# Keys and values as seven half-size products from the fourth attention unit on, the input sums two at a time in the first two units, and lambda folded into the scaling of the second softmax map

## The chip, the cores and the metric

The kernel runs on one core of one Trainium2 chip. The metric is the device time of one execution in microseconds. The kernel before takes 712.08 us, the median of 3 runs (711.63 to 712.46).

## The reference, cut to what matters

The block has 528 positions (16 meta tokens and 512 of the sequence), a width of 1024 and float32 data. A layer norm gives `h`; one projection `w_in` gives queries, keys, values and gates of two attention branches:

```python
proj = jnp.einsum('bld,dn->bln', h, w_in[i])
q_d, k_d, v_d, g_d, q_s, k_s, v_s, g_s, m_d, m_s = jnp.split(proj, IN_OFFSETS, axis=-1)
# differential attention: 8 heads, two softmax maps each
p = jax.nn.softmax(s, axis=-1)
a = p[:, :, 0] - lam * p[:, :, 1]
y_d = jnp.einsum('bhqk,bhkd->bhqd', a, v)
# stick-breaking attention: 16 heads, products of (1 - sigmoid) from the right
```

The two branches are normed, gated, projected, merged by sigmoid gates, projected once more and normed with the residual. Only the keys and values of the two branches and the line `a = ...` are touched here.

## The kernel before

**Numbers as pairs.** Each float32 operand of a large product is split into a high part, rounded to the matmul's format, and a low part, the rest. ScalarE (ACT) writes the high part of a weight tile (`wh`, L183), VectorE (DVE) the low part (`wl`, L188), and TensorE (PE) adds three products: high by high, high by low, low by high. A weight item is a tile of 128 x 4 x 128 and costs one ACT and one DVE instruction on 512 columns. `prep` does that for the item that is four ahead of the one that TensorE is to use.

**Units.** Attention goes through 16 units, u = 0 to 15: the 8 differential heads, then 8 pairs of stick-breaking heads. While the attention of unit u runs, TensorE also projects the keys and values of unit u+1 and the queries of unit u+2, so that small attention products and long projections lie between each other. A query (or gate) projection is 24 matmuls on 512 columns (L494 to L496).

**Two ways to the keys and values.** Up to the unit `SEVEN - 1` the keys (`stage_k`) and the values (`stage_v`) of a unit are two plain projections: 2 halves of the positions x 8 slices x 3 products each, 96 matmuls on 264 columns in all (L510). From unit `SEVEN` on `stage_kv` computes both together: the 2 x 2 blocks of (keys, values) by (first, second half of the positions) come from seven half-size products in place of eight, as in Strassen's scheme in Winograd's form: 7 x 4 x 3 = 84 matmuls on 264 columns (L690), with some sums before and behind them. Its weight sums are made by DMAs of GpSimd (POOL) that add into the tiles `rawk` (L146) and by one DVE addition (L169); it prepares seven weight items in place of four.

**Input sums.** The seven products also need four sums of the blocks of `h`. `input_sums(k)`, k = 0 to 3, makes a quarter of them: one small POOL copy (L660), four DVE operations on 264 columns (L662 to L665, in the tiles `hF`), one ACT cast into `tS` (L667) and one DVE subtraction on 1056 columns into `tl` (L668). The second of the seven products reads all four quarters of `tS` and `tl`. Before, with `SEVEN = 5`, the quarters are made one in each of the units u = 0 to 3, and the first seven products run in u = 4.

**Scores of a differential head.** For each of the 4 query blocks, last block first, and each of the two maps, TensorE fills a score bank `sc` (L754; there are two such banks), DVE adds the bias, takes the minimum and moves the scores to the map's tile `e` (L834), and ACT takes the exponential and its row sum `zs` (L838). Then DVE takes the reciprocals `rz` (L842), multiplies that of the second map by `nlam`, which is -lambda (L843, one column), scales the first map (L844) and adds the scaled second map to it (L845), which gives `apad`. TensorE transposes `apad` (L766, into `t`), ACT and DVE split the transposes (`ah`, `al`), and TensorE multiplies by the values (`av`).

**What sets the order.** Inside a unit `run(proj, steps)` walks through the projections and calls each step when the walk has come to the step's time (a number such as 8.0 on a scale of some 15 a unit). From u = 0 up to the end of the attention that is the order in which instructions are written, not the order in which they are issued: a scheduler places them afterwards, engine by engine, by its own estimate of when each is ready, and each engine then works through its list in that order. `placed` ties a few of them to the instructions written just before.

Of the kernel before, what the change touches and what calls it, by code (L numbers as in the profile page):

```python
# [35 lines left out]

ORDERED = [mybir.EngineType.PE, mybir.EngineType.DVE, mybir.EngineType.Activation, mybir.EngineType.Pool]
WARM = 14
SEVEN = 5
TD = [(0.85, 11.0, 14.5), (0.95, 13.0, 16.5)]  # L40
GATE_AT = {4: 0, 5: 1, 6: 2, 7: 3, 8: 4, 11: 5, 14: 6}
LO, HI = slice(0, 64), slice(64, 128)
# [3 lines left out]
def hybrid_block_kernel(ctx: ExitStack, tc: tile.TileContext, x, meta, emb_g, emb_b, w_in, b_gate,  # L46
# [175 lines left out]
    def placed(work, engines=ORDERED):  # L222

        ins = nc.cur_bb.bb.instructions
        n = len(ins)
        work()
        for e in engines:
            new = next((i for i in ins[n:] if i.engine == e), None)
            old = next((ins[m] for m in range(n - 1, max(n - 400, 0), -1) if ins[m].engine == e), None)
            if new is not None and old is not None:  # L230
                follow(new, old)
# [349 lines left out]
    with tc.tile_pool(name="att", bufs=1) as ap:  # L581
# [75 lines left out]
        def input_sums(k):  # L657


            g.tensor_copy(hP[k][:, :, :M], hM[:, k:k + 5:4])  # L660
            b11, b12, b21, b22 = [hP[k][:, m, ts(n, H2)] for m in range(2) for n in range(2)]
            v.tensor_tensor(b22, b12, b22, op=ALU.subtract)  # L662
            v.tensor_tensor(b12, b11, b12, op=ALU.subtract)
            v.tensor_tensor(b11, b22, b11, op=ALU.subtract)
            v.tensor_tensor(b21, b11, b21, op=ALU.add)  # L665
            h, l = tS[0][:, k:k + 5:4], pair_of("tl", F32R)
            s.copy(h, hP[k])  # L667
            v.tensor_tensor(l, hP[k], h.bitcast(F32), op=ALU.subtract)  # L668
            tL.append(l)
# [139 lines left out]
        def d_scores(unit, h):  # L809

            A = unit["A"]


            bias = ap.tile([P, L], F32, tag="bias", name="bias", bufs=2)
            if h == 0:
                g.iota(bias, pattern=[[-1, L]], base=400, channel_multiplier=1, allow_small_or_imprecise_dtypes=True)
                g.affine_select(bias, bias, pattern=[[-1, L]], compare_op=ALU.is_ge, fill=1e30, base=400,
                                channel_multiplier=1)
            g.tensor_scalar(bias, biases[-1] if h else bias, 0.5 if h else -0.5, None, op0=ALU.mult)
            biases.append(bias)  # L820
            a = apads[h % 2]
            mn = ap.tile([P, NB, 2, 2], F32, tag="mn", name="mn", bufs=2)
            zs = ap.tile([P, NB, 2], F32, tag="zs", name="zs", bufs=2)
            rz = ap.tile([P, NB, 2], F32, tag="rz", name="rz", bufs=2)
            for i in reversed(range(NB)):
                nk = NKEY[i]
                e = [E[c][:, ZOFF[i]:ZOFF[i] + nk] for c in range(2)]
                for c in range(2):
                    m = mn[:, i, c, :]
                    for n, (ps, k0, use) in enumerate(logits(A[c], K[c], i)):  # L830
                        if n == 1:
                            yield
                        b0 = 384 - P * i + k0
                        v.tensor_tensor_reduce(e[c][:, k0:k0 + use], ps[:, :use], bias[:, b0:b0 + use], -1.0, 3e38,  # L834
                                               ALU.add, ALU.min, m[:, n:n + 1])
                    if nk > 512:
                        v.tensor_tensor(m[:, 0:1], m[:, 0:1], m[:, 1:2], op=ALU.min)
                    s.activation(e[c], e[c], AF.Exp, scale=-1.0, bias=m[:, 0:1], accum_out=zs[:, i, c:c + 1])  # L838
                    if c == 0:
                        yield  # L840
                r = rz[:, i, :]
                v.reciprocal(r, zs[:, i, :])  # L842
                v.tensor_scalar(r[:, 1:2], r[:, 1:2], nlam, None, op0=ALU.mult)  # L843
                v.tensor_scalar(e[0], e[0], r[:, 0:1], None, op0=ALU.mult)  # L844
                v.scalar_tensor_tensor(a[:, AOFF[i]:AOFF[i] + nk], e[1], r[:, 1:2], e[0], op0=ALU.mult, op1=ALU.add)  # L845
                yield

        def d_values(unit, ta):
# [105 lines left out]
        for u, (kind, n) in enumerate(UNITS):  # L954
            unit = units[u]
            if u + 3 == SEVEN:
                pools["rawk"] = ap
            last = u + 1 == len(UNITS)
            proj = [] if last else keys_values(units[u + 1], *UNITS[u + 1])
            if u + 2 < len(UNITS):  # L960
                proj.append(stage_q(units[u + 2], *UNITS[u + 2]))
            steps = pending + [(0.6, lambda unit=unit: values(unit, kind))]
            pending = []
            if u + 1 < SEVEN:
                steps.append((9.2, store_k))
            if u in range(SEVEN - 5, SEVEN - 1):
                if not tS:
                    tS.append(ypool.tile([P, KT, L], F32R, tag="ys", name="tS"))
                steps.append((8.0, lambda k=u + 5 - SEVEN: placed(lambda: input_sums(k))))
            if u in GATE_AT and u < 14:  # L970
                proj.append(raw_gate(GATE_AT[u], kept["r"][GATE_AT[u]]))
            if kind == "d":
                ta = {}
                dt, t0, t1 = TD[u in GATE_AT]
                steps += spread(d_scores(unit, n), 0.0, dt, 10)
                parts = transposed(ta, apads[n % 2])
                steps += [(t0 + 0.7 * m, f) for m, f in enumerate(parts)]
                steps.append((t1, lambda: d_values(unit, ta)))
                pending = [(3.0 if n < 7 else 5.8, lambda unit=unit, n=n: d_norm(unit, n))]
            else:  # L980
                if n == 0:
                    diag.append(ap.tile([P, L], F32, tag="bias", name="diag", bufs=2))
                    g.memset(diag[0], 0.0)
                    g.tensor_copy(diag[0][:, L - P:], ident)
                    g.memset(v3[:, 1], 0.0)
                    for a in apads:
                        for i in range(NB):
                            g.memset(a[:, ds(AOFF[i] + NKEY[i] - 1, 1)], 0.0)
                if last:
                    ydT = [pair_of("ydT", n=S) for k in range(4)]  # L990
                    ydT = [ydT[k % 4][:, k // 4, :] for k in range(8)]
                    ysT = ypool.tile([P, 8, S], F32, tag="ys", name="ysT")
                    ysT = [ysT[:, k, :] for k in range(8)]
                    unit["y"] = ysT[7]

                    def fill_in(y, of):
                        placed(lambda: nc.sync.dma_start(y, of), [mybir.EngineType.SP])

                    fill_in(ydT[7], kept["d"][7])
                    for m, (y, of) in enumerate(((ydT, "gd"), (ysT, "gs"))):  # L1000
                        for j in range(7):
                            steps.append((1.3 + 1.5 * (7 * m + j), lambda o=y[j], x=kept[of][j]: fill_in(o, x)))
                    proj += [gate("d", n, lambda: ydT[7]), merge_gate(0, 0), merge_gate(0, 1), merge_gate(0, 2),
                             gate("s", n, lambda: ysT[7])]
                else:
                    if GATE_AT.get(u) == n:
                        yd = gpool.tile([P, S], F32, tag="sg", name="yd")
                        nc.sync.dma_start(yd, kept["d"][n])
                        proj.append(gate("d", n, lambda yd=yd: yd, kept["gd"][n]))
                    else:  # L1010
                        steps += zip((12.0, 24.0), late_gate(ap, *(kept[x][n] for x in ("d", "r", "gd"))))
                    proj.append(gate("s", n, lambda unit=unit: unit["y"], kept["gs"][n]))
                for c in range(2):
                    ta = {}
                    steps += spread(s_scores(unit, c, n == 0), (2.0 + 4.3 * c) if n == 0 else 4.4 * c, 0.85, 5)
                    parts = transposed(ta, apads[c])
                    times = LAST[c] if last else [7.0 + 6.5 * c + 0.7 * m for m in range(3)] + [10.5 + 6.5 * c]
                    steps += zip(times, parts)
                    steps.append((times[3], lambda c=c, ta=ta: s_values(unit, c, n, ta)))
                if last:  # L1020
                    steps.append((LAST[0][0] - 0.1, lambda: state.update(ends=len(nc.cur_bb.bb.instructions))))
            run(proj, steps)
# [236 lines left out]
```

## Time and profile before

| | before |
|---|---|
| median of 3 runs | 712.08 us |
| the profiled execution: its own time | 712.22 us |
| the profiled execution: span from first to last instruction | 710.4 us |
| granted TensorE clock, mean | 0.995 |
| busy in the span: PE, DVE, ACT, POOL | 697.5, 571.8, 439.2, 125.6 us |
| start of the units u = 1, 2, 3, 4, 5 on TensorE (first matmul of the next unit's keys) | 59.49, 83.54, 107.59, 131.66, 159.79 us |

A row of instruction groups gives line, engine, operation, output and inputs, shape, count, then busy time, the mean duration of one in ns, and the idle time of the engine just before. A row of stretches gives for each engine the busy time and the count, then the granted clock, the share of the DMA engines' time and GB/s. A row of the timeline gives start, duration, engine, line, operation, names, shape and count. A duration reaches from an instruction's start to its end; on TensorE and VectorE the next one starts before that end, so what an instruction costs in a dense stretch is the step from start to start.

### The profile page before, as it was taken

To read this page: it belongs to the slowest core of one execution; us is meant where nothing else is said; L and a number is where in the kernel's file an instruction comes from. 1 tells how busy PE (TensorE), PEld (TensorE's weight loads), DVE (VectorE), ACT (ScalarE), POOL (GpSimd) and SP (SyncE) were. 2 spreads that over 40 slices of the span, in tenths; PEclk is the share of its full clock that TensorE was granted. 3 is DMA by queue.
4 is the path that set the end of the run, shared out by engine and by line. 5 is a ranking of instruction groups with operands and counts; after the bars stand their busy time and mean duration, and the time that the engine had idled before them with its cause. 6 is when DMAs were issued, how large, how long until landed. Compare 5 with 4: busy or idle time off the path is not lost.

```text
span 710.4 us, 13389 instructions
## 1 busy us (share of the span) xinstructions
PE 697.5 (98%) x4494; PEld 636.9 (90%) x4494; DVE 571.8 (80%) x1265; ACT 439.2 (62%) x1065; POOL 125.6 (18%) x143
## 2 busy tenths in 40 slices
PE   9999999999999999999999999999999999999994
PEld 8999999989999898988989998988889998999884
DVE  6888897878787777988878889976666788788897
ACT  5766676757667587776857777666455546455300
POOL 3214210212222111212123120000012102220002
PEclk9999999999999999999999999999999999999997
DMA  9368754879888876899897976646576748795902
GB/s 293 93 169 164 167 133 125 184 181 183 198 200 184 201 177 164 186 215 214 200 217 174 206 171 175 166 133 197 178 174 112 164 123 182 133 198 170 322 15 104
DMA packets 182182, 123.36 MB, mean 174 GB/s; under 512 B 9009, under 2 KB 165074, under 8 KB 182114
## 3 DMA queue, kind: packets, MB, share of 16 engines
q1 hardware_dynamic: 148130, 102.32, 50.1%
q0 software_dynamic: 33664, 19.14, 21.6%
q10 hardware_dynamic: 320, 1.06, 0.4%
q8 instruction: 35, 0.57, 0.3%
q14 instruction: 33, 0.27, 0.1%
HBM read 91.96 MB, written 9.44 MB: 143 GB/s over the span
## 4 chain that ended last, share of the span: by engine, by line
PE 86%; DVE 6%; DMA 3%; ACT 2%; issue 1%; POOL 1%; SPq 0%; ACTq 0%; DVEq 0%; POOLq 0%
PE q L690 16%; PE ps L496 12%; PE ps L494 12%; PE ps L495 12%; PE q L1065 10%; PE ps L510 7%; PE sc L754 6%; PE t L766 4%; DMA lgb<-in_ln_b_dram 1%; PE bank L385 1%; PE tv L723 1%; DVE hr L1215 1%; DMA xt<-in_x_dram 1%; PE av L922 1%; DMA raw<-in_w_out_dram 1%
## 5 line engine op out<-in xcount | busy, mean ns | idle before, releaser
L188 DVE TENSOR_TENSOR wl<-raw,wh 128x512 fp32r<-128x512 f32 x169 | 115.7, 691 | 43.7 <-ACT wh L183 42.2
L494 PE MATMUL ps<-hTh,wh 128*128 128x512 f32 x368 | 145.0, 394 | 0.0
L495 PE MATMUL ps<-hTl,wh 128*128 128x512 f32 x368 | 144.5, 393 | 0.0
L496 PE MATMUL ps<-hTh,wl 128*128 128x512 f32 x368 | 144.4, 392 | 0.0
L183 ACT CAST wh<-raw 128x512 fp32r<-128x512 f32 x169 | 104.4, 625 | 28.0 <-PE ps L495 15.3
L496 PEld LDWEIGHTS ps<-hTh,wl 128*128 128x128 f32 x368 | 69.2, 188 | 13.9
L495 PEld LDWEIGHTS ps<-hTl,wh 128*128 128x128 f32 x368 | 69.2, 188 | 13.1
L494 PEld LDWEIGHTS ps<-hTh,wh 128*128 128x128 f32 x368 | 69.2, 188 | 12.9
L146 POOL DMA_DIRECT2D rawk<-in_w_in_dram x44 | 60.8, 1642 | 96.9 <-DMA rawk<-in_w_in_dram 58.4
L754 PE MATMUL sc<-k,A 128*128 128x264 f32 (+3 forms) x320 | 65.9, 299 | 0.1
L1065 PE MATMUL q<-gh,wh 128*128 128x256 f32 x224 | 63.5, 283 | 0.2 <-ACT t L1074 0.2
L1065 PE MATMUL q<-gl,wh 128*128 128x256 f32 x224 | 63.4, 283 | 0.0
L1065 PE MATMUL q<-gh,wl 128*128 128x256 f32 x224 | 63.4, 283 | 0.0
L907 DVE TENSOR_TENSOR_SCAN e<-e,diag 128x528 f32<-128x528 f32 (+1 forms) x64 | 53.4, 848 | 7.5 <-ACT e L901 7.3
L754 PEld LDWEIGHTS sc<-k,A 128*128 128x128 f32 x320 | 50.3, 189 | 3.3 <-ACT e L901 0.3
L690 PE MATMUL q<-tS,wh 128*128 128x264 f32 x176 | 50.9, 290 | 0.9 <-DVE low L612 0.9
L690 PE MATMUL q<-tl,wh 128*128 128x264 f32 x176 | 50.2, 286 | 0.0
L690 PE MATMUL q<-tS,wl 128*128 128x264 f32 x176 | 50.2, 286 | 0.0
L510 PE MATMUL ps<-hTh,wh 128*128 128x264 f32 x160 | 46.4, 290 | 0.2 <-ACT k L632 0.2
L933 POOL DMA_DIRECT2D ys<-half x14 | 11.8, 840 | 195.9 <-ACT ys L932 119.2
L510 PE MATMUL ps<-hTh,wl 128*128 128x264 f32 x160 | 45.6, 286 | 0.0
L510 PE MATMUL ps<-hTl,wh 128*128 128x264 f32 x160 | 45.5, 285 | 0.0
(291 smaller groups left out, 1851.4 us busy)
## 6 DMA issues: line engine op xcount, KB each, us to landing
raw<-in_w_in_dram SPq DMA_DIRECT2D x141, 256.0 KB, 3.3
rawk<-in_w_in_dram POOLq DMA_DIRECT2D x44, 256.0 KB, 6.0
rawk<-in_w_in_dram SPq DMA_DIRECT2D x33, 256.0 KB, 3.9
k<-ks SPq DMA_DIRECT2D x60, 132.0 KB, 3.1
raw<-in_w_out_dram SPq DMA_DIRECT2D x16, 256.0 KB, 3.9
k<-ks SPq DMA_DIRECT2D x60, 66.0 KB, 2.8
A<-low SPq DMA_DIRECT2D x28, 128.0 KB, 2.8
raw<-in_w_br_diff_dram SPq DMA_DIRECT2D x12, 256.0 KB, 4.7
```

The lines of the kernel that those rows point to most:

```text
L146: second[l] = [lambda raw=raw, x=x: g.dma_start(raw, x, accum_op=ALU.add) for x in more]
L183: s.copy(wh, raw)
L188: eng.tensor_tensor(wl, raw, wh.bitcast(F32), op=ALU.subtract)
L494: pe.matmul(ps, wh[:, k % 4, :], hTh[:, k, M:], start=(k == 0), stop=False)
L495: pe.matmul(ps, wh[:, k % 4, :], hTl[:, k, M:], start=False, stop=False)
L496: pe.matmul(ps, wl[:, k % 4, :], hTh[:, k, M:], start=False, stop=(k == KT - 1))
L510: pe.matmul(ps[:, :H2], a[:, k % 4, :], b[:, k, ts(c, H2)], start=(k == 0 and m == 0), stop=(k == KT - 1 and m == 2))
L690: pe.matmul(bank, a[:, k, :], b, start=start and k == 0 and j == 0, stop=k == 3 and j == 2, skip_group_check=not start)
L754: pe.matmul(ps[:, :n], q, K[:, m, k0:k0 + n], start=(m == 0), stop=(m == 1))
L766: pe.transpose(t[:, o:o + P], a[:, AOFF[i] + j * P:AOFF[i] + (j + 1) * P], ident)
L907: v.tensor_tensor_scan(rev, rev, diag[0][:, L - nk:][:, ::-1], 0.0, ALU.mult, ALU.max)
L1065: pe.matmul(bank, a[:, k, :], b[:, n, k, :], start=start and k == 0 and m == 0, stop=k == 3 and m == 2, skip_group_check=not start)
```

## The change

`SEVEN` goes from 5 to 3: the keys and values of units 3 and 4 come from seven products too, so that the first seven products run in u = 2. The input sums are made two in u = 0 and two in u = 1, at 8.0 and 12.5 on the scale of the unit. In the scores, the second map is scaled by one operation with two factors (its reciprocal and `nlam`), and the first map is scaled in the addition; the one-column multiplication is gone.

```diff
-SEVEN = 5
+SEVEN = 3
...
                 v.reciprocal(r, zs[:, i, :])
-                v.tensor_scalar(r[:, 1:2], r[:, 1:2], nlam, None, op0=ALU.mult)
-                v.tensor_scalar(e[0], e[0], r[:, 0:1], None, op0=ALU.mult)
-                v.scalar_tensor_tensor(a[:, AOFF[i]:AOFF[i] + nk], e[1], r[:, 1:2], e[0], op0=ALU.mult, op1=ALU.add)
+                v.tensor_scalar(e[1], e[1], r[:, 1:2], nlam, op0=ALU.mult, op1=ALU.mult)
+                v.scalar_tensor_tensor(a[:, AOFF[i]:AOFF[i] + nk], e[0], r[:, 0:1], e[1], op0=ALU.mult, op1=ALU.add)
                 yield
...
             if u + 1 < SEVEN:
                 steps.append((9.2, store_k))
-            if u in range(SEVEN - 5, SEVEN - 1):
+            if u + 1 < SEVEN:
                 if not tS:
                     tS.append(ypool.tile([P, KT, L], F32R, tag="ys", name="tS"))
-                steps.append((8.0, lambda k=u + 5 - SEVEN: placed(lambda: input_sums(k))))
+                steps += [(8.0 + 4.5 * k, lambda k=2 * u + k: placed(lambda: input_sums(k))) for k in range(2)]
```

The scheduler makes new lists of all engines from this. First TensorE in u = 2. Before, the head of that unit's list reads (`ps` is the bank of the keys' plain projection, `sc` a score bank of unit 2, `t0` and `t1` transposes of unit 1; tiles carry their numbers):

```order
L510 MATMUL ps_1313<-hTh_149,wh_1112 128x264
L754 MATMUL sc_1330<-k0_448,A0_962 128x264 x2
L754 MATMUL sc_1334<-k0_448,A0_962 128x264 x2
L510 MATMUL ps_1313<-hTl_150,wh_1112 128x264
L510 MATMUL ps_1313<-hTh_149,wl_1113 128x264
L510 MATMUL ps_1313<-hTh_149,wh_1112 128x264
L510 MATMUL ps_1313<-hTl_150,wh_1112 128x264
L510 MATMUL ps_1313<-hTh_149,wl_1113 128x264
L766 MATMUL t0_1226<-ident_129,apad1_434 128x128 x4
L784 MATMUL t1_1238<-ident_129,sx_1224 128x128
L766 MATMUL t1_1238<-ident_129,apad1_434 128x128 x3
L510 MATMUL ps_1313<-hTh_149,wh_1112 128x264
```

Two score banks, and then projection matmuls again; the other scores of the unit follow one or two at a time up to its end. Now, a little behind the same place (the first of these rows comes after three quarters of the second of the seven products):

```order
L852 MATMUL av_1304<-ah0_1246,V_1018 128x512
L754 MATMUL sc_1444<-k0_448,A0_979 128x400 x2
L766 MATMUL t2_1270<-ident_129,apad1_434 128x128 x3
L754 MATMUL sc_1455<-k1_449,A1_980 128x400 x2
L754 MATMUL sc_1479<-k0_448,A0_979 128x272 x2
L723 MATMUL tv_1361<-ident_129,vT_1128 128x128 x4
L754 MATMUL sc_1501<-k1_449,A1_980 128x272 x2
L754 MATMUL sc_1515<-k0_448,A0_979 128x144 x2
L853 MATMUL av_1304<-af3_1278,v3_436 128x128
```

No projection matmul lies between these. The piece goes on with the other products by the values, and ends so (`q_1335` and `q_1336` are banks of the seven products, `ms` the norm of unit 1, `tl_1288` the last quarter of the input sums):

```order
L727 MATMUL t4_1367<-ident_129,sx_1368 128x128
L754 MATMUL sc_1537<-k1_449,A1_980 128x144 x2
L690 MATMUL q_1335<-tS_631,wh_1183 128x264
L875 MATMUL ms_1432<-sqh_1319,onesm_142 128x512
L876 MATMUL ms_1432<-sql_1320,onesm_142 128x512
...
L690 MATMUL q_1336<-hTh_149,wl_1292 128x264
L690 MATMUL q_1335<-tl_1288,wh_1183 128x264
```

From the first score bank of unit 2 (`sc_1351`) to the matmul that reads `tl_1288` stand all the 10 score banks, transposes and products of one unit's attention, but only 20 matmuls of the seven products: 7 behind `sc_1351`, one ahead of the norm, and 12 behind it.

On VectorE the last quarter of the input sums stood before in u = 3, a unit ahead of the first seven products (`hF_178` are its blocks, `tl_1883` its result, `sc_1829` to `sc_1858` scores of unit 3):

```order
L665 TENSOR_TENSOR hF_178<-hF_178 128x264
L834 ISA e1_447,mn_1682<-sc_1829,bias_1680 128x272
L834 ISA mn_1682 128x1
L732 TENSOR_TENSOR V_1700<-tv_1695,V_1700 128x384
L736 TENSOR_TENSOR v4_435<-t4_1701,v4_435 128x128
L870 TENSOR_TENSOR sql_1655<-sq_1652,sqh_1654 128x512
L612 SCALAR_TENSOR_TENSOR low_1663<-ps_1566,A0_1661 128x512
L668 TENSOR_TENSOR tl_1883<-hF_178,tS_631 128x1056
```

Now it stands in u = 2, behind all the scores of that unit (`sc_1537` is the tenth of its ten score banks):

```order
L665 TENSOR_TENSOR hF_178<-hF_178 128x264
L844 SCALAR_TENSOR_TENSOR apad0_433<-e0_446,rz_1350,e1_447 128x400
L843 TENSOR_SCALAR e1_447<-e1_447,rz_1350,nlam_146 128x272
L834 ISA e1_447,mn_1348<-sc_1537,bias_1346 128x144
L834 ISA mn_1348 128x1
L732 TENSOR_TENSOR V_1366<-tv_1361,V_1366 128x384
L736 TENSOR_TENSOR v4_435<-t4_1367,v4_435 128x128
L869 TENSOR_TENSOR sql_1320<-sq_1317,sqh_1319 128x512
L612 SCALAR_TENSOR_TENSOR low_1328<-ps_1230,A0_1326 128x512
L844 SCALAR_TENSOR_TENSOR apad0_433<-e0_446,rz_1350,e1_447 128x272
L668 TENSOR_TENSOR tl_1288<-hF_178,tS_631 128x1056
```

The steps of u = 1 at 8.0 and 12.5 thus lie a unit apart on VectorE: those of the third quarter in u = 1, together with those of the second, which were written in u = 0, and those of the fourth in u = 2.

## The prediction

> **What bounds the kernel now.** I read the page first: the span, the engines' shares, and the chain of work that ended last.
>
> ```profile
> span 710.4 us, 13389 instructions
> PE 697.5 (98%) x4494; PEld 636.9 (90%) x4494; DVE 571.8 (80%) x1265; ACT 439.2 (62%) x1065; POOL 125.6 (18%) x143
> PE 86%; DVE 6%; DMA 3%; ACT 2%; issue 1%; POOL 1%; SPq 0%; ACTq 0%; DVEq 0%; POOLq 0%
> ```
>
> TensorE is busy for 98% of the span and holds 86% of the chain. A busy TensorE can still hide waits, so I looked at stretches next, one for each of the units u = 1, 2, 3 (stretch, length, then busy time and count of PE, PEld, DVE, ACT, POOL, then clock, DMA share, GB/s).
>
> ```profile
> 59.49:83.54 24.05, 24.05 (x172) 22.82 (x171) 19.97 (x61) 16.00 (x43) 7.47 (x7) 1.00 0.83 159
> 83.54:107.59 24.05, 24.05 (x172) 22.83 (x171) 20.31 (x61) 16.36 (x43) 3.11 (x2) 1.00 0.76 167
> 107.59:131.66 24.07, 24.07 (x172) 22.83 (x171) 20.73 (x62) 16.38 (x43) 3.13 (x2) 1.00 0.56 141
> ```
>
> Three units with the same matmuls take the same 24.05 us to 0.02, without an idle moment of TensorE, while the other engines' load differs. So TensorE's own list is the bound in these units, VectorE has about 4 us of 24 to spare, and ScalarE 8. Last, the timeline, for what one matmul costs in a dense stretch: the first and the last row of 25 projection matmuls on 264 columns in a row, and of 11 on 512 columns.
>
> ```profile
> 121.41 0.28 PE L510 MATMUL ps<-hTl,wh 128*128 128x264 f32 x1
> ...
> 124.31 0.28 PE L510 MATMUL ps<-hTl,wh 128*128 128x264 f32 x1
> ...
> 129.17 0.39 PE L495 MATMUL ps<-hTl,wh 128*128 128x512 f32 x1
> ...
> 131.44 0.39 PE L496 MATMUL ps<-hTh,wl 128*128 128x512 f32 x1
> ```
>
> 24 steps take 2.90 us, 0.121 each, though one matmul shows 0.28 from start to end; 10 steps on 512 columns take 2.27, 0.227 each.
>
> **The matmuls that go.** Units 3 and 4 have 84 matmuls on 264 columns in place of 96: 24 fewer, which at 0.121 is 2.90 us. They lie on the engine that sets the time, so all of it counts, if TensorE doesn't wait for something new.
>
> **What the seven products add elsewhere.** Each of the two units gets three more weight items (a cast on ACT, a subtraction on DVE), one DVE sum, some three more DVE operations on 264 columns, and loses its input sum.
>
> ```profile
> L183 ACT CAST wh<-raw 128x512 fp32r<-128x512 f32 x169 | 104.4, 625 | 28.0 <-PE ps L495 15.3 <-PE q L690 4.3 <-PE ps L510 2.4
> L169 DVE TENSOR_TENSOR rawk<-rawk,raw 128x512 f32<-128x512 f32 x11 | 7.5, 683 | 0.0
> ...
> L188 DVE TENSOR_TENSOR wl<-raw,wh 128x512 fp32r<-128x512 f32 x12 | 8.6, 723 | 3.9 <-ACT wh L183 3.9
> L668 DVE TENSOR_TENSOR tl<-hF,tS 128x1056 fp32r<-128x1056 f32 x2 | 2.5, 1252 | 0.0
> L636 DVE TENSOR_TENSOR ks<-ps,ks 128x264 fp32r<-128x264 f32 x4 | 1.7, 425 | 0.0
> L843 DVE TENSOR_SCALAR rz<-rz,nlam 128x1 f32<-128x1 f32 x8 | 1.7, 208 | 0.1
> L844 DVE TENSOR_SCALAR e<-e,rz 128x528 f32<-128x528 f32 x2 | 1.1, 526 | 0.0
> L662 DVE TENSOR_TENSOR hF<-hF 128x264 f32<-128x264 f32 x2 | 0.9, 426 | 0.0
> ```
>
> On DVE: 3 x 0.72 + 0.68 + 3 x 0.43 = 4.1 us more, less an input sum of 4 x 0.43 + 1.25 = 3.0, less 4 x 0.21 = 0.8 for the one-column multiplications: 0.3 us more in units of 24.05 - 1.45 = 22.6 us that have 20.3 to 20.7 of work. ACT gets 3 x 0.63 = 1.9 on 16.4. Both fit beside TensorE: nothing, with 1.5 us of cover on DVE.
>
> **Lambda in the scaling.** The 32 one-column multiplications go, and the scaling has two factors in place of one. The nearest row of DVE with two factors is that of the first norm, on 512 columns:
>
> ```profile
> L335 DVE TENSOR_SCALAR xn<-xt,xmv,xrs 128x512 f32<-128x512 f32 x7 | 3.5, 533 | 2.0 <-POOL xrs L297 2.0
> ```
>
> 533 ns against 526 on 528 columns with one factor: the same. At worst it costs what the addition behind it does, 0.24 us more on 528 columns. Per unit it is at best 0.8 us less on an engine that TensorE doesn't wait for: nothing by itself.
>
> **Where the input sums go.** This is the term that decides. Before, the last quarter was ready long before it was read (its row on VectorE, and the first matmul that reads any of the sums):
>
> ```profile
> 124.18 1.26 DVE L668 TENSOR_TENSOR tl<-hF,tS 128x1056 fp32r<-128x1056 f32 x1
> ...
> 133.61 0.29 PE L690 MATMUL q<-tS,wh 128*128 128x264 f32 x1
> ```
>
> 125.44 to 133.61 is 8.2 us of lead. In the new lists the last quarter (`tl_1288`) stands on VectorE behind all the scores of unit 2, and on TensorE 20 projection matmuls behind the first of these scores. Each engine works in order, so two sums start at the same point, the score bank `sc_1351`, and end at the same point, the matmul that reads `tl_1288`.
>
> TensorE between them: one unit's attention and 20 matmuls. A unit of 24.05 us has 96 x 0.121 = 11.62 of keys and values and 24 x 0.227 = 5.45 of queries, which leaves 6.98 for its attention; with 20 x 0.121 = 2.42 that is 9.40, less two score matmuls (0.24) before the start: 9.2 us.
>
> VectorE between them: everything that it does in a unit such as u = 1 (19.97 us), the input sum with it, but for five of the six weight subtractions, two key evictions, the last block's scaling, addition and reciprocal, and the four one-column multiplications. The rows that are not quoted yet:
>
> ```profile
> L842 DVE RECIPROCAL rz<-zs 128x2 f32<-128x2 f32 x8 | 1.3, 157 | 0.9 <-ACT e L838 0.9
> ...
> L845 DVE SCALAR_TENSOR_TENSOR apad<-e,rz,e 128x144 f32<-128x144 f32 x2 | 0.7, 360 | 0.0
> ...
> L844 DVE TENSOR_SCALAR e<-e,rz 128x144 f32<-128x144 f32 x2 | 0.6, 310 | 0.0
> ```
>
> 5 x 0.72 + 2 x 0.43 + 0.36 + 0.31 + 0.16 + 4 x 0.21 = 6.1 us by whole durations. But the next one starts before the end, as the timeline of u = 1 shows:
>
> ```profile
> 75.50 0.68 DVE L612 SCALAR_TENSOR_TENSOR low<-ps,A 128x512 fp32r<-128x512 f32 x1
> 76.10 1.25 DVE L668 TENSOR_TENSOR tl<-hF,tS 128x1056 fp32r<-128x1056 f32 x1
> 77.26 0.30 DVE L834 CUSTOM_DVE_ANT_0 e<-sc,bias 128x144 f32<-128x144 f32 x1
> ```
>
> Steps of 0.60 and 1.16 for 0.68 and 1.25: 0.08 less each, 1.1 us for 14. So the stretch is 13.9 to 15.0 us of dense VectorE work; I take 14.4, the middle. TensorE has 9.2 to do in that time and cannot go on: it waits 5.2 us (4.7 to 5.8), and as the rest of the kernel is its own dense list, this is never made up.
>
> To that come VectorE's own waits. In u = 1 they were these:
>
> ```profile
> DVE wl L188 <- ACT wh L183: 2.0, 2, 1.2
> DVE ax L788 <- PE t L766: 0.8, 1, 0.8
> DVE al L772 <- ACT ah L771: 0.3, 1, 0.3
> ```
>
> The last two kinds are in the stretch: up to 1.1 us. And VectorE may come late to `sc_1351`: u = 1 now has two input sums, 19.97 + 3.0 + 0.7 - 0.8 = 22.9 us, which with all three waits (3.1) is 26.0 in 24.05: up to 1.9 us late. Both are nearer to nothing, since a fuller list has shorter waits; I take 1.0 for them and the hand-overs. The wait is 6.2 us, between 4.7 and 8.8. Behind `tl_1288` VectorE's list holds weight work only, ahead of its use: no second wait.
>
> The sum, against the profiled execution: 712.22 - 2.90 + 6.2 = 715.5 us, a span of 713.7. That execution was 0.14 above the median of its runs, so I forecast 715.4, with 713.9 to 718.0 as this case's own range.
>
> **The rivals.** *The clock falls in the wait.* The granted clock at the end of the span, and TensorE's start:
>
> ```profile
> 698.00:702.00 4.00, 2.68 (x23) 2.47 (x21) 3.45 (x7) 0.00 (x0) 1.06 (x2) 1.00 0.28 109
> 702.00:706.00 4.00, 0.00 (x0) 0.00 (x0) 3.81 (x10) 0.51 (x1) 1.27 (x3) 0.61 0.21 79
> ...
> 1.43 5.82 PE L306 MATMUL warm<-ident 128*128 128x128 f32 x28 [1.43 <-POOL ident masks.py:199]
> ...
> 8.51 0.61 PE L306 MATMUL warm<-ident 128*128 128x128 f32 x4
> ```
>
> The last matmul ended at 700.7; a mean of 0.61 between full and half puts the fall at 702.9, 2.2 us later. At the start 28 matmuls took 5.8 us, 0.21 each, later four took 0.61. Here TensorE's wait is cut up by scores that VectorE lets in one by one, but its last piece, from `sc_1537` until the last quarter is cast and subtracted, can be 2 to 3 us with little in it. If the clock falls, up to 5.8 us of matmuls run at half rate, a loss of 0 to 2.9; I take 1.5, which gives 716.9.
>
> [...]
>
> *TensorE is not held (faster).* If VectorE reached `tl_1288` within 9.2 us of `sc_1351`, the order would cost nothing, and the 24 matmuls would show alone: 709.2. For it speaks that VectorE has 4 us to spare in a unit; against it, that 14.4 us of listed work would have to shrink by a third. *Half of it:* a stretch of 11 to 13 us of VectorE, a wait of 1.5 to 4.3, 710.7 to 713.5, no change.
>
> *The sums come later still.* The last quarter begins with a POOL copy that stands behind seven of POOL's adding DMAs (six before, but two units later), and u = 1 has a DMA share of 0.83 already.
>
> ```profile
> rawk<-in_w_in_dram POOLq DMA_DIRECT2D x44, 256.0 KB, 6.0
> ```
>
> One landing of 6.0 us late, of which 4 hidden by the scores ahead of it, is 2 us more; two are 8: 717.4 to 723. For it speaks little: before, the same queue kept nobody waiting.
>
> **How the numbers follow.** The forecast has 0.54, the clock 0.28, the later sums 0.05, the half 0.06, TensorE not held 0.07. About 0.2% (1.4 us) is what a measurement can tell from no change. Slower is 0.54 + 0.28 + 0.05 = 0.87, same 0.06, faster 0.07. The range takes the forecast's from 713.6, a little below its lower bound, and reaches into the clock's case to 718.6; faster, same and the late sums (0.18) lie outside.
>
> **What would show it.** Right: a stretch of about 15 us at the start of u = 2 (some 83 to 100 us) in which TensorE has 9 us of work, with waits for VectorE and for the last cast into `tS`, VectorE dense in it; u = 2 takes about 29 us (22.6 + 6.2) and u = 3 22.6; elsewhere the steps stay at 0.121 and 0.227. The clock's rival shows as granted clock under 1.00 there. Wrong: no gap of TensorE in u = 2, or gaps in other units, or waits for `rawk` and POOL.

## The result, and the profile after

The changed kernel takes 720.84 us, the median of 6 executions (719.55 to 722.50), against 712.43 for the kernel before in the same runs (6 executions, 711.63 to 712.82): a ratio of 1.0121, 95% interval 1.0111 to 1.0131. The forecast was 715.4 and the range ended at 718.6. The sign was right, and the loss is more than twice what was forecast. The profiled execution took 719.55 us, the fastest of the six.

The page of the changed kernel, its span, the engines' shares and the chain:

```profile
span 717.7 us, 13390 instructions
PE 699.7 (97%) x4470; PEld 636.2 (89%) x4470; DVE 577.3 (80%) x1247; ACT 442.8 (62%) x1073; POOL 137.0 (19%) x151
PE 81%; DVE 9%; ACT 3%; issue 3%; DMA 3%; POOL 1%; SPq 0%; ACTq 0%; DVEq 0%; POOLq 0%
```

TensorE has 24 instructions fewer and shows 2.2 us more of busy time; its share of the chain falls by 5 points, and VectorE's rises by 3. Stretches of the changed kernel (length, then busy time and count of PE, PEld, DVE, ACT, POOL, then clock, DMA share, GB/s): the units u = 1, 2 and 3, the stretch from behind `sc_1351` to the matmul that reads `tl_1288`, and three pieces around its end.

```profile
59.56:83.62 24.06, 24.06 (x172) 22.80 (x171) 21.14 (x60) 15.82 (x41) 3.72 (x2) 1.00 0.53 130
83.62:113.50 29.88, 26.24 (x161) 22.77 (x159) 25.37 (x71) 20.42 (x53) 6.79 (x5) 0.94 0.61 144
113.50:135.67 22.17, 22.17 (x157) 20.97 (x155) 16.79 (x46) 14.73 (x37) 5.13 (x4) 1.00 0.93 193
85.56:100.98 15.42, 11.78 (x71) 9.54 (x70) 15.10 (x50) 12.15 (x34) 5.46 (x4) 0.95 0.72 136
96.10:99.52 3.42, 1.88 (x9) 1.26 (x10) 3.42 (x10) 2.57 (x7) 2.20 (x2) 1.00 0.61 76
99.52:102.93 3.41, 3.41 (x17) 3.41 (x17) 3.39 (x8) 2.83 (x7) 0.00 (x0) 0.50 0.53 154
102.93:106.34 3.41, 3.41 (x27) 3.22 (x26) 2.21 (x5) 1.81 (x4) 0.00 (x0) 1.00 0.57 170
```

u = 1 is what it was, with one input sum more on VectorE. u = 2 takes 29.88 us in place of 24.05, and VectorE is busy for 15.10 of the 15.42 us of the fourth row: the hold. Right behind it the clock is halved for 3.41 us, with 17 matmuls where the same time behind it has 27. u = 3 takes 22.17, as 12 fewer matmuls should make it (22.6 by the forecast; it has 157 matmuls in place of 172, so three more have moved out of it). TensorE's timeline in the hold (start, duration, and in brackets the idle time before and what ended it):

```profile
85.32 0.66 PE L754 MATMUL sc<-k,A 128*128 128x264 f32 x4
...
90.95 0.63 PE L723 MATMUL tv<-ident,vT 128*128 128x128 f32 x4 [0.37 <-DVE al L772]
...
92.38 0.45 PE L754 MATMUL sc<-k,A 128*128 128x144 f32 x2 [0.52 <-DVE mn L834]
...
94.52 0.42 PE L754 MATMUL sc<-k,A 128*128 128x144 f32 x2
97.37 0.39 PE L690 MATMUL q<-tS,wh 128*128 128x264 f32 x1 [2.43 <-ACT tS L667]
...
99.66 0.42 PE L690 MATMUL q<-hTh,wh 128*128 128x264 f32 x1
99.88 0.42 PE L690 MATMUL q<-hTl,wh 128*128 128x264 f32 x1
...
100.98 0.42 PE L690 MATMUL q<-tl,wh 128*128 128x264 f32 x1
```

The scores come one by one as VectorE lets them in; behind the last of them TensorE stands for 2.43 us until ScalarE has cast the last quarter. From 99.66 the steps are 0.22 in place of 0.12. VectorE's subtraction in the same place:

```profile
99.04 1.25 DVE L668 TENSOR_TENSOR tl<-hF,tS 128x1056 fp32r<-128x1056 f32 x1
```

It ends at 100.29, 14.7 us behind `sc_1351`. TensorE's waits in the whole span (engine, line, releaser: total, times, longest) have, beside those of the hold, one kind that the kernel before did not have:

```profile
PE q L690 <- ACT tS L667: 2.4, 1, 2.4
...
PE sc L754 <- DMA k<-ks: 0.7, 2, 0.4
...
PE sc L754 <- DVE mn L834: 0.5, 1, 0.5
PE tv L723 <- DVE al L772: 0.4, 1, 0.4
```

Scores now wait for the transfers that store the next unit's keys (`k<-ks`, L643 and L644). The two key tiles, one for each map, exist once. Their new contents come from eight transfers of SyncE (SP), four for each tile; the last of a tile's can begin when the last score of the unit that reads this tile has done so. The first score of a unit reads the first map's tile, and that tile is read last by the ninth of the unit's ten score banks. Their rows in the page's list of transfers (KB of one, median us from issue to landing):

```profile
k<-ks SPq DMA_DIRECT2D x60, 132.0 KB, 3.3
...
k<-ks SPq DMA_DIRECT2D x60, 66.0 KB, 3.0
```

How far apart these two scores stand in TensorE's list is seen in the timelines. Before, at the change from unit 3 to unit 4 (the ninth bank of unit 3 and the first scores of unit 4; at the three changes ahead of it the distance is 6.6 to 7.8 us):

```profile
124.43 0.34 PE L754 MATMUL sc<-k,A 128*128 128x144 f32 x2
132.28 0.65 PE L754 MATMUL sc<-k,A 128*128 128x264 f32 x4
```

After, at the same place:

```profile
135.79 0.34 PE L754 MATMUL sc<-k,A 128*128 128x144 f32 x2
139.62 0.49 PE L754 MATMUL sc<-k,A 128*128 128x264 f32 x2 [0.40 <-DMA k<-ks]
```

7.8 us of distance were left before, 3.8 are left now, with a wait of 0.40 in them. It is the only change of keys at which the new list leaves less than the 6.6 us that were the least before. In this execution the waits for stores cost little, in others more, as the experiments show.

**Where 7.3 us of span come from.** I compared each step of TensorE, from start to start, with the usual step of its kind (the median of the steps of that shape), and summed the excess by stretches of 20 us: it is 9.9 us larger after than before. Of these, 5.9 lie between 80 and 100 us (the hold), 1.3 between 100 and 120 (mostly the halved clock), 0.7 between 120 and 140 (mostly the key stores) and 2.0 in small pieces behind. 9.9 - 2.9 = 7.0; the other 0.3 of the 7.3 lie behind the last matmul.

### The profile page after: what moved, and what is told of

Read it like the earlier page. It is cut to its first block, busy times and chain, and to the rows that moved or that the text cites. A ratio compares the mean times of both kernels' runs of the same rounds, so it can differ in the third digit from the quotient of the medians.

```text
span 717.7 us, 13390 instructions
## 1 busy us (share of the span) xinstructions
PE 699.7 (97%) x4470; PEld 636.2 (89%) x4470; DVE 577.3 (80%) x1247; ACT 442.8 (62%) x1073; POOL 137.0 (19%) x151
## 4 chain that ended last, share of the span: by engine, by line
PE 81%; DVE 9%; ACT 3%; issue 3%; DMA 3%; POOL 1%; SPq 0%; ACTq 0%; DVEq 0%; POOLq 0%
PE q L690 17%; PE ps L495 11%; PE ps L494 11%; PE ps L496 11%; PE q L1064 10%; PE sc L754 5%; PE ps L510 4%; PE t L766 3%; DMA lgb<-in_ln_b_dram 1%; PE bank L385 1%; PE warm L306 1%; PE tv L723 1%; DMA raw<-in_w_out_dram 1%; DVE hr L1214 1%; PE av L921 1%
## 5 line engine op out<-in xcount | busy, mean ns | idle before, releaser
L183 ACT CAST wh<-raw 128x512 fp32r<-128x512 f32 x167 | 102.9, 625 | 28.7 <-PE ps L495 16.3
L146 POOL DMA_DIRECT2D rawk<-in_w_in_dram x52 | 72.1, 1627 | 129.4 <-DMA rawk<-in_w_in_dram 59.6
L690 PE MATMUL q<-tS,wh 128*128 128x264 f32 x208 | 60.6, 292 | 3.4 <-ACT tS L667 2.4
L690 PE MATMUL q<-tl,wh 128*128 128x264 f32 x208 | 59.6, 287 | 0.0
L690 PE MATMUL q<-tS,wl 128*128 128x264 f32 x208 | 59.6, 288 | 0.0
L183 ACT CAST wh<-rawk 128x512 fp32r<-128x512 f32 x52 | 32.3, 621 | 23.9 <-PE ps L495 13.0
L772 DVE TENSOR_TENSOR al<-t,ah 128x512 fp32r<-128x512 f32 (+2 forms) x72 | 39.4, 550 | 7.8 <-ACT ah L771 5.6
L690 PE MATMUL q<-hTh,wh 128*128 128x264 f32 x156 | 45.4, 291 | 0.1
```

What stands on the lines that cost most here:

```text
L146: second[l] = [lambda raw=raw, x=x: g.dma_start(raw, x, accum_op=ALU.add) for x in more]
L183: s.copy(wh, raw)
L690: pe.matmul(bank, a[:, k, :], b, start=start and k == 0 and j == 0, stop=k == 3 and j == 2, skip_group_check=not start)
L772: v.tensor_tensor(l, t[:, o:o + w], h.bitcast(F32), op=ALU.subtract)
```

## The experiments

The theory after the result: the price has three parts, the hold of u = 2, a stretch at half clock that it causes (3.41 us in the profile), and a second hold, scores that wait for key stores, because the new lists shorten that distance here and there. Rivals: the seven products or the new scaling cost by themselves; the sums are too much work for the early units wherever they stand; what came on top of the hold is scattered and has no cause of its own.

### The same sums, six units of the scale earlier

```diff
-                steps += [(8.0 + 4.5 * k, lambda k=2 * u + k: ...
+                steps += [(2.0 + 4.5 * k, lambda k=2 * u + k: ...
```

> The whole change, but the two input sums of a unit are called at 2.0 and 6.5 on its scale in place of 8.0 and 12.5. In the new lists the last quarter then stands on VectorE ahead of the scores of unit 2, and no clump of scores without projections is left on TensorE. Theory (TensorE is held in u = 2 because the last quarter comes too late, and the clock falls in that wait): both losses go, the 24 matmuls show, 712.4 - 2.9 = 709.5 us; up to 2 us more if the later units' new lists cost something. Rival (the seven products of units 3 and 4 cost more on VectorE, ScalarE and the DMAs than their matmuls save, wherever the sums stand): 716 us or more, with TensorE waiting in u = 2 to 4. Second rival (the sums' load in u = 0 and 1 holds TensorE): waits in u = 0 and 1, 713 to 716 us.

Measured: 711.11 us (12 executions, 709.43 to 712.25), ratio to before 0.9982 (0.9973 to 0.9990). Its units u = 1 and u = 2:

```profile
60.19:84.21 24.02, 24.02 (x173) 22.79 (x171) 22.14 (x63) 16.66 (x45) 3.15 (x2) 1.00 0.62 152
84.21:106.77 22.56, 22.56 (x161) 21.34 (x159) 21.20 (x61) 17.23 (x44) 6.81 (x5) 1.00 0.85 174
```

u = 2 takes 22.56 us, without an idle moment of TensorE and at full clock. So the price of the hold is neither the seven products nor the number of sums, only when the last quarter comes. Of the 2.9 us that 24 matmuls are worth, 1.3 to 1.4 arrive. The trace has one wait of a score for a key store, 0.4 us.

### The clock kept up by work in the wait

```diff
+                    if h == 2 and i == 0 and c == 1:
+                        for _ in range(9):
+                            pe.matmul(ps[:, 256:384], ident, ident, start=True, stop=True)
```

Nine matmuls that nobody reads, behind unit 2's last score bank.

> The changed kernel with nine matmuls that nobody reads, of identity by identity, behind the tenth score bank of unit 2, in free columns of its bank: they fill some 1.9 of the 2.6 us in which TensorE had nothing to do there. The lists are otherwise those of the changed kernel at this place. Theory (part of the loss is the half clock after that wait): the granted clock stays at 1.00 throughout, and the time falls by 1.7 us (one window at half rate) to 3 us (where other executions lost more than the profiled one): 718 to 719 us, with less spread between runs. Rival (the fall of the clock costs nothing, since TensorE waits for the last quarter anyway, or the spread has another cause): 720.8 us as the changed kernel, or more by the nine matmuls.

Measured: 723.96 (4 executions, 720.95 to 724.26). The profiled one, 720.95, kept the full clock to the last matmul (mean 0.997), and still was no faster than the change. The other three show a mean clock of 0.991 to 0.994 and took 723.88 to 724.26: the added matmuls did not keep the clock up in each execution. The waits of the profiled one:

```profile
PE sc L754 <- DMA k<-ks: 1.9, 2, 1.4
PE sc L838 <- DVE mn L834: 1.9, 1, 1.9
```

The hold is there (now in front of the added matmuls), and the waits for key stores are longer than in the change's profile. The expectation of 718 to 719 us missed, and what the halved clock costs is not shown by this run: the term that it had left out, the waits for stores, moves by as much as the clock is worth. The run without key stores, further below, has the same hold without the halved clock and shows it better.

### The sums alone, in the kernel before

The two lines of the change on the sums, with `SEVEN = 5`:

```diff
-            if u in range(SEVEN - 5, SEVEN - 1):
+            if u < 2:
...
-                steps.append((8.0, lambda k=u + 5 - SEVEN: ...
+                steps += [(8.0 + 4.5 * k, lambda k=2 * u + k: ...
```

> The kernel before (seven products from unit 5 on, old scaling), with only the input sums moved as in the change: two in u = 0 and two in u = 1, called at 8.0 and 12.5. Theory (what costs is the deadline, not the load: nobody reads the sums before u = 4): the time of the kernel before, 712.4 us, within 1 us. Rival (two sums in a unit overload VectorE and hold TensorE in u = 1 and 2): 715 us or more, with TensorE waiting in u = 1 or 2.

Measured: 713.26 (11 executions, 712.46 to 715.66), ratio 1.0014 (1.0002 to 1.0025), and no wait of TensorE for `tS` or `tl` in its trace. The sums' load costs some 1 us; it is the use in u = 2 that makes them late. In the trace one score, at 163.39 us, waits 0.7 us for a key store, which none did in the profile of the kernel before: a new order alone can bring such a wait.

### The change with the old scaling

```diff
-                v.tensor_scalar(e[1], e[1], r[:, 1:2], nlam, op0=ALU.mult, op1=ALU.mult)
-                v.scalar_tensor_tensor(a[:, ...], e[0], r[:, 0:1], e[1], ...)
+                v.tensor_scalar(r[:, 1:2], r[:, 1:2], nlam, None, op0=ALU.mult)
+                v.tensor_scalar(e[0], e[0], r[:, 0:1], None, op0=ALU.mult)
+                v.scalar_tensor_tensor(a[:, ...], e[1], r[:, 1:2], e[0], ...)
```

> The changed kernel with the old scaling of the two maps (the one-column multiplication is back, 32 times). The clump of TensorE in u = 2 is the same in its list; VectorE has three such multiplications of 0.13 us a step more between the two ends of the wait. Theory (the scaling is not the cause, its relief of VectorE is hidden but for the stretch in u = 2): 720.8 to 722 us, 0 to 1 us slower than the changed kernel. Rival (the new order of the scaling, which ends with the first map, is part of the loss): 718 us or less.

Measured: 722.95 (4 executions, 722.62 to 723.66), 2.1 more than the change and 1 us above the range of the theory. The rival, that the new scaling is part of the loss, falls. Between the ninth bank of unit 3 and the first score of unit 4 its list leaves 2.9 us beside the wait (3.4 in the change); TensorE there:

```profile
135.94 0.35 PE L754 MATMUL sc<-k,A 128*128 128x144 f32 x2
...
141.72 0.77 PE L754 MATMUL sc<-k,A 128*128 128x264 f32 x2 [2.90 <-DMA k<-ks]
142.28 0.42 PE L690 MATMUL q<-tS,wh 128*128 128x264 f32 x1
```

and SyncE, which issues the stores:

```profile
136.20 0.47 SPq L644 DMA_DIRECT2D k<-ks  x1
136.76 0.62 SPq L643 DMA_DIRECT2D k<-ks  x1
137.47 0.56 SPq L614 DMA_DIRECT2D A<-A  x1
138.13 1.35 SPq L644 DMA_DIRECT2D k<-ks  x1
```

The second hold in full: a score waits 2.90 us for a store, and the clock halves behind it (granted 0.50 from 141.74 to 145.15 us; 0.42 for a duration of 0.28). The score needs the two stores that SyncE issues at 136.20 and 136.76, right behind the ninth bank. They landed at 140.01 and 141.58 by the trace, 3.8 and 4.8 us after their issue, where this run's page has medians of 3.0 and 3.1 for their sizes. A distance of 2.9 us is less than a usual store takes, and this one took longer.

### The change once more

> The changed kernel once more, for a second profile, since its executions lay between 719.6 and 722.5 us and the first profile is of the fastest. In TensorE's list 3.0 us of work stand between the last score of unit 3 that reads the first map's keys and the first score of unit 4 that reads the new ones (6.4 to 14.3 us at all such places before); the stores of the new keys have to land in between. Theory (there is a second hold, the key stores at the start of u = 4, of varying length): a time above the first profile's 719.6 goes with a longer wait of scores for key stores near 139 us, 0.6 us in the first profile, up to 3 us, and maybe a second fall of the clock. Rival (only the first hold and its clock vary): the wait near 139 us stays at 0.6 us and the half-rate stretch near 100 us is longer.

Measured: 722.6 us. Its waits, and the two longest of them in the timeline:

```profile
PE sc L754 <- DMA k<-ks: 3.6, 4, 1.5
PE q L690 <- ACT tS L667: 2.4, 1, 2.4
```

```profile
62.03 0.73 PE L754 MATMUL sc<-k,A 128*128 128x264 f32 x4 [1.49 <-DMA k<-ks]
...
349.40 0.48 PE L754 MATMUL sc<-k,A 128*128 128x264 f32 x2 [1.25 <-DMA k<-ks]
```

The same program, 3.05 us slower than the other profile, and the waits of scores for key stores are 2.9 us longer: this is where these two executions differ. None of the four waits stands at the change to unit 4, where I had expected them.

At 62.03, the first score of unit 1, a short distance is not the cause either: beside the wait the list leaves 6.7 us there, as the kernel before does (6.6). The store came late. By the traces it was issued at 54.02 and landed at 56.40 in the kernel before, at 54.41 and 59.21 in the first profile of the change, at 56.09 and 61.90 here. Between 46 and 62 us the DMA engines are fuller than before (mean share 1.22 against 0.63), and a key store took 4.9 or 5.8 us to land (medians of the two sizes; 5.7 and 4.8 in the first profile) against 2.0 and 2.4. The profiles of this case go together in that: 2.0 to 2.4 us with seven products from unit 5 on, 3.3 and 3.4 from unit 4 on, 3.4 to 5.8 from unit 3 on. The weights of the first seven products are fetched and summed in this stretch when these run in u = 2; POOL's first adding DMA starts at 35.7 us in place of 56.7. That this load delays the stores is the likely reading, which no run tests by itself. At 349.40 the distances are 18 us and more, as in the kernel before; why that store came late is open.

### Two versions between

The sums at 5.0 and 9.5 in both units:

```diff
-                steps += [(8.0 + 4.5 * k, lambda k=2 * u + k: ...
+                steps += [(5.0 + 4.5 * k, lambda k=2 * u + k: ...
```

> The whole change, but the sums are called at 5.0 and 9.5. No clump is left in u = 2, but TensorE's list has only 3.8 us between the last score of unit 3 on the first map's keys and the first score of unit 4 (8.1 us with the sums at 2.0 and 6.5). Theory of two holds: no wait for the sums, but scores wait for key stores at the start of u = 4 by 0.5 to 2 us: 711 to 713 us, 0.5 to 2 us over the version with the sums at 2.0 and 6.5. Theory of one hold (the sums alone): the time of that version, 711.1 us, or less.

Measured: 712.87 (10 executions, 711.88 to 713.69), ratio 1.0002 (0.9993 to 1.0012). No hold in u = 2; three waits of 0.7 to 0.8 us stand in later units, by the profile for VectorE and ScalarE. One of them, 0.79 us at 132.88, is that of the first score of unit 4, where the theory of two holds had put it. The profile names VectorE's `yd` (L886) there, which this score does not read; it needs the key stores issued at 128.85 and 129.49, so that it most likely waited for these. The time is in that theory's range, 711 to 713.

Three sums in u = 0 and the last at 2.0 in u = 1:

```diff
+                steps += [(t, ...) for t, q in ([(1.0, 0), (5.0, 1), (9.0, 2)] if u == 0 else [(2.0, 3)])]
```

> The whole change, but three quarters of the sums are called in u = 0 (at 1.0, 5.0 and 9.0) and the last in u = 1 (at 2.0). No clump, and at least 6.6 us in TensorE's list at all changes of keys. Theory of two holds: neither occurs, the 24 matmuls show: 709.5 to 711 us. Rival (the sums' load in u = 0 holds TensorE): waits in u = 0, 713 us or more.

Measured: 714.95 (8 executions, 712.93 to 716.52), ratio 1.0037 (1.0024 to 1.0050): a miss by 4 us. Its early units are as fast as those of the version with the sums at 2.0. Then, in the profiled execution (716.52, the slowest of the eight), a score waits for a key store at 342 us, and the clock halves behind it:

```profile
342.08 0.94 PE L754 MATMUL sc<-k,A 128*128 128x264 f32 x4 [2.54 <-DMA k<-ks]
```

```profile
339.27:342.68 3.41, 0.87 (x7) 0.68 (x6) 0.69 (x1) 0.97 (x3) 0.00 (x0) 1.00 0.56 144
342.68:346.10 3.42, 3.42 (x16) 3.23 (x15) 2.16 (x3) 2.27 (x6) 0.00 (x0) 0.50 0.95 283
```

A change in u = 0 can show 340 us later, since the scheduler makes all later lists anew.

### The scaling alone

The three lines of the change on the scaling, in the kernel before.

> The kernel before with the new scaling alone (lambda as a second factor, the one-column multiplication gone). Theory: VectorE's relief of 0.5 us a unit is hidden behind TensorE: 712.4 us, within 1 us either way by the new lists. Rival (the scaling shortens the path of the scores, or lengthens it): 711 us or less, or 714 us or more, with TensorE's waits gone or new.

Measured: 711.83 (10 executions, 711.51 to 712.58), ratio 0.9991 (0.9982 to 1.0001). Nothing, as forecast, or a little less.

### Without the key stores

In the changed kernel, in the kernel before, and in the version with the sums at 2.0, the same line:

```diff
             keys(1, x)
-            store_k()
+            staged.clear()
```

> The changed kernel without the key stores behind the seven products: the eight transfers into the two key tiles are left out in each of the units 2 to 14, so that the scores of units 3 to 15 are computed with the keys of unit 2. No score can wait for a store then, while the scores and products between the first score bank and the last quarter of the sums in u = 2 stand in the list as in the change. Theory (the miss is a second hold, scores that wait for key stores): the hold of u = 2 and one window at half clock stay, the waits of scores for transfers go: 712.4 - 2.9 + 6.0 + 1.4 = 716.9, range 716 to 718. Rival (what came on top is scattered and has nothing to do with the stores): 719.5 to 721.5, as the change.

> The kernel before without the key stores behind its seven products (the scores of units 5 to 15 are computed with the keys of unit 4), as the control of the run without stores of the change. The trace of before shows no score that waits for a store. Theory and rival alike: 712.4, within 0.7; a larger gain would say that leaving out the stores helps by itself, and would have to be taken off what it brings in the change.

> The change with the sums at 2.0 and 6.5, without the key stores behind the seven products (the scores of units 3 to 15 are computed with the keys of unit 2). With the stores this version gained 1.4 us of the 2.9 that 24 fewer matmuls are worth. Theory (what is missing are scores that wait for stores too): 709.5 to 710.2. Rival (the missing 1.5 us lie in the start and the end of the run, or in the lists, not in stores): 710.8 to 711.3.

Measured, against before at 712.43 (27 executions):

| without the key stores | median us (executions) | ratio to before, 95% | with them |
|---|---|---|---|
| the change | 715.83 (5) | 1.0048 (1.0031 to 1.0065) | 720.84 |
| the kernel before | 711.33 (11) | 0.9986 (0.9976 to 0.9995) | 712.43 |
| sums at 2.0 and 6.5 | 710.90 (11) | 0.9974 (0.9962 to 0.9987) | 711.11 |

The change loses 5.0 us of its time, the kernel before 1.1 (more than the 0.7 that was expected at most), the early version 0.2. The waits of the change without the stores:

```profile
PE q L690 <- ACT tS L667: 2.4, 1, 2.4
...
PE q L690 <- DVE low L612: 0.9, 2, 0.6
PE sc L754 <- DVE mn L834: 0.5, 1, 0.5
PE tv L723 <- DVE al L772: 0.4, 1, 0.4
```

The hold of u = 2 stands as it was. Its excess between 80 and 120 us is 6.0 us, against 7.2 in the change: the profiled execution had no stretch at half clock there (granted 1.00, where the change has 0.50 for 3.41 us), and the 1.2 us between these two executions of the same hold are what that stretch costs. What depends on the stores is 5.0 us of the change's 8.4, or 3.9 if the control's 1.1 is taken off. In the profiled executions 1.3 of the control's 2.0 us lie behind the last matmul (8.8 us from its start to the end, against 10.0 in the kernel before), and there the change gained nothing (10.3 with and without stores), so that 3.9 is rather too low. That is more than waits alone: without stores the lists of the later units are made anew too, and the clock had its part. The rival, 719.5 to 721.5 as the change, falls; the share of waits, lists and clock is not told apart by this.

For the early version the rival was right: leaving out the stores brings it nothing, so the 1.5 us that it is short of 2.9 are not lost there. In its trace the excess is spread over many places; that stays open.

### Half of the change

`SEVEN = 4`, two sums in u = 0 at 4.0 and 10.0, one each in u = 1 and u = 2 at 8.0, the new scaling.

> Half of the change: the seven products from unit 4 on (12 fewer matmuls, 1.45 us), two quarters of the sums in u = 0 at 4.0 and 10.0, one each in u = 1 and u = 2 at 8.0, the new scaling. The sums are there a unit ahead of their use, and the lists keep 5.7 us and more between the last score on a key tile and the first of the next unit. Theory (deadline of the sums, distance of the key stores): no hold, 712.4 - 1.45 = 711.0, range 710.6 to 711.7. Rival (seven products in an early unit cost by themselves): 712.4 or more.

Measured: 711.67 (11 executions, 711.04 to 712.75), ratio 0.9988 (0.9979 to 0.9998): no hold, and 0.8 of 1.45 us. The best version is the one with the sums at 2.0 and 6.5, 0.18% below the kernel before.

## Why the prediction was too low

- **24 fewer matmuls, -2.90 us.** They go: u = 3 takes 22.17 us and, with early sums, u = 2 takes 22.56, where 22.6 was forecast. The condition, that TensorE doesn't wait for something new, failed. Even the version without a hold keeps only half of the 2.9 at the end, and why is open.
- **Where the input sums go, a wait of 6.2 us.** Right in mechanism, place and size. VectorE's part, from `sc_1351` to the end of `tl_1288`, took 14.7 us (forecast 14.4 and 1.0 for its own waits); TensorE's excess from 80 to 100 us is 5.9 us.
- **The clock.** I took "the clock falls in the wait" for a rival, at 1.5 us and 0.28. In the change it is a part of the price, not an alternative: the clock halved behind the hold in both profiles, for 1.2 to 1.3 us. All six executions of the change show a mean clock of 0.991 to 0.994, those of the kernel before mostly 0.995 to 0.997. The row that I had read for it, a fall 2.2 us behind the last matmul at the end of the span, was the right warning, and I gave it too little weight. With the fall alone the time would still have been inside the range.
- **"No second wait": the step that failed.** I looked for a second wait only behind `tl_1288` on VectorE's list, and put the load of the seven products at nothing after counting VectorE and ScalarE alone. The second wait is for SyncE's stores of the keys, for which scores wait in both profiles of the change, in that with the added matmuls and in that with the old scaling: 0.7 us of named waits in the first profile of the change, 3.6 in the second, 1.9 and 2.9 in the other two. The run without stores puts what depends on them at 3.9 to 5.0 us of the median. Two things make stores late: the new list shortens the distance at the change to unit 4 from 7.8 us to 3.8, and in the first units the stores take longer to land (medians of 4.8 and 5.7 us between 46 and 62 us, against 2.4 and 2.0 before). Their shares are not told apart.
- **Lambda in the scaling, nothing.** Right: 711.83 against 712.4 by itself.
- **The sum.** For the first profile it closes: 712.2 - 2.9 + 5.9 (hold) + 1.3 (clock) + 0.7 (stores at the change to unit 4) + 2.0 (small pieces, other waits for stores among them) + 0.3 (behind the last matmul) = 719.5, measured 719.55. The median is 1.3 us above that; the second profile, whose waits for stores are longer by as much as it is slower, says where such a difference comes from. By the run without stores, 712.4 - 2.9 + 6.0 for the hold and 3.9 to 5.0 for the stores give 719.4 to 720.5 of the 720.84; these 3.9 to 5.0 hold a part of the clock's price. The forecast alone would have been 715.4.

## What to carry to other kernels

An order that a scheduler makes anew has a distance for every tile that is refilled in place, and each of them can become too short; list all of them ahead of summing one, and ask whether the refilling transfers still land in the time that they took before. Once a hold of several microseconds is forecast, the halved clock behind it belongs into the sum with a chance of its own: here 3.4 us at half clock came on top of the hold in both profiles of the change, for 1.2 to 1.3 us, and none in the profile without key stores, which has the same hold. And when a step becomes due can matter more than how much work it saves: the same sums, six units of the scale earlier, stand here for 9.7 us, the saved matmuls for 2.9.

## What the runs showed of the hardware

By the clock records of the first profile, the clock of the change is full from 7.36 to 99.52 us, that is for 92.160 us, at half for 3.413, and full again for 607.572, up to the fall behind the last matmul. By those of the kernel before it is full from 6.55 to 702.87, for 696.319 us, up to that fall. The three full stretches are 27, 178 and 204 times 3.4133 us, so the length of the stretch at half clock fits into each of them a whole number of times. In the other profiles with a fall inside the span the clock was at 0.50 for 3.42 us in the second profile of the change (from 99.60), for 6.83 and 3.41 with the old scaling (from 97.36 and 141.74), and at least for 3.42 in the version with three sums in u = 0 (from 342.68).

TensorE was not idle in the 3.4 us ahead of these falls. In the change they have 1.88 of 3.42 us busy by the profile (the row 96.10:99.52 above), and the longest idle piece was 2.43 us; in the second profile of the change 0.98 us are busy, with the old scaling 0.99 and 0.52, and 0.87 in the version with three sums. The change without stores has the same hold, with the same wait of 2.4 us, and two stretches of that length in it were busy a little longer:

```profile
92.93:96.34 3.41, 1.95 (x14) 1.67 (x13) 3.41 (x12) 2.71 (x9) 1.00 (x1) 1.00 0.62 77
96.34:99.76 3.42, 2.19 (x11) 1.57 (x12) 3.42 (x9) 2.57 (x6) 1.89 (x2) 1.00 0.62 77
99.76:103.17 3.41, 3.41 (x26) 3.14 (x25) 3.41 (x9) 3.14 (x9) 0.00 (x0) 1.00 0.53 154
```

The clock stayed full. At the end of the span, the last 3.4 us ahead of the fall have 1.22 us busy in the kernel before (699.46:702.87) and 0.57 in the change (707.09:710.51). So these profiles have falls behind 0.52 to 1.88 busy microseconds, and none behind the 1.95 and 2.19 of the hold without stores. No run varies the busy time alone, so why the one hold was paid twice and the other was not is not shown.
